# Accumulator tiles for four up products, later Gelus and a later second softmax, and gate multiplications left to the scheduler, in a PEER decoder layer

## The chip, the cores and the metric

The kernel runs on one core of a Trainium2 chip. The metric is the device time of one execution in microseconds, taken as the median of the runs.

## The reference

One hybrid decoder layer over 256 tokens with 16 meta tokens ahead of them and a width of 2048, all in float32. The token-mixing half is a layer norm, an input projection, a causal pooling mixer, a gated short convolution, a gated merge and an output projection. The channel-mixing half is a PEER layer, which retrieves single-neuron experts by product keys; the change concerns this half alone:

```
q = (xb @ w_q).reshape(PEER_BLOCK, PEER_HEADS, 2, PEER_HALF)
s1 = einsum("thc,hnc->thn", q[:, :, 0], keys_1)
s2 = einsum("thc,hnc->thn", q[:, :, 1], keys_2)
v1, i1 = top_k(s1, 16)
v2, i2 = top_k(s2, 16)
...
top_s, sel = top_k(cand_s, 16)
gate = softmax(top_s)
act = gelu(einsum("td,tkd->tk", xb, expert_u[idx]))
coef = gate * act
return einsum("tk,tkd->td", coef, expert_v[idx])
```

There are 128 x 128 = 16384 experts, 8 heads, and 16 experts for each head and token.

## The kernel before

The kernel does not gather expert rows for most tokens. For the first TD = 224 tokens it multiplies all 16384 experts with the tokens and weights each product with a gate, which is zero for an expert that the token did not choose. The experts come in 128 groups of 128, and `e` counts the groups. The last 32 tokens are computed from gathered rows ("lone" rows).

**Splitting.** A float32 weight tile `raw` (1 MB, three buffers) comes by a DMA that SyncE (SP) issues (`load`, L82 to L85). In two halves it is split into a rounded part `whi` (a cast on ACT, L95) and a rest `wlo` (a subtraction, L74, on DVE or POOL); each has three buffers. TensorE (PE) multiplies both parts.

**up(e)** (L627) is the first product, of group e's rows of expert_u with the 224 tokens: 32 matmuls (L108, L109) into one PSUM tile of the pool `mm`, which has four buffers and also serves the query products, the transposes and the gate products. Afterwards `both` (L111) copies one half of the result to `gl` (ACT, L112) and adds the other (DVE, L113). The Gelu (ACT, L625) is put off: `gelus(late)` leaves the `late` newest tiles for later. The first LEAD = 44 ups run ahead of the second products; both their `wlo` halves are made by POOL.

**The gates.** The query products are finished by `q_done`, which finds the top 16 on DVE (lines 438 to 512). `finish(t)` (L514) makes the softmax of token tile t: a subtraction (DVE, L522), an Exp (ACT, L526), a sum, a reciprocal and a multiplication (DVE, L531), and then three PE transposes (L545). It is begun after the ups that ROUTED names and goes on by one step at every half up. Then `gates` builds one-hot matrices on DVE and multiplies them on PE (L595), and a copy of the gates goes to memory (`spill`), 7 pieces of 32 tokens.

**The down phase** has 32 blocks of NB = 4 groups (the loop at L782). For a block, `fetch` (L742) reads its gates `G` back with 7 DMAs of 64 KB on SP's queue, into one of two buffers. `coef(e)` (L644) multiplies `gl` with `G` (DVE, L648) and splits it into `c_hi` (ACT, L77) and `c_lo` (DVE, L74). `down(es, dh)` multiplies with two 1 MB tiles of expert_v for each half dh of the output: 48 matmuls for 4 groups (L660). Two further ups stand ahead of each `down` until all 128 are done, so the last blocks run without ups. The gathers of lone rows lie in between.

**What sets the order.** A tile framework schedules the program by priorities and by the order in which it is written; each engine and each DMA queue then runs its instructions in one fixed order. Two statements steer it: `tc.high_priority(offset)` pulls the casts ahead, and `tc.issue_after(instruction)` binds an instruction behind another that stands earlier on its engine. `last_on["dve"]` is the latest `wlo` or `both` addition on DVE.

Of the kernel before, what the change touches and what calls it, by code (L numbers as in the profile page):

```python
# [35 lines left out]
NB = 4  # L36
NBLK = NKEY // NB
AHEAD = 80
UAHEAD = 100
LEAD = 44  # L40
ROUTED = (3, 6)
GT = 8
TG = 32
LONE = 32
TD = T - LONE
# [8 lines left out]
def block(ctx, tc, x, meta, w_in, small, pool_w, projs, w_out, wq, keys, eu, eur, ev,  # L54
          ln1_g, ln1_b, ln2_g, ln2_b, lin_g, lin_b, out):
    nc = tc.nc
# [10 lines left out]
    def ps_mm():  # L67
        return mm.tile([P, 512], F32, name="mm")

    def ps_acc(t, c):  # L70
        return accp.tile([P, 512], F32, name=f"acc{t}{c}")
# [4 lines left out]
    def split(hi, lo, full):  # L76
        nc.scalar.copy(hi, full)  # L77
        lo_part(lo, full, hi)
# [3 lines left out]
    def load(src, shape=None):  # L82
        t = raws.tile([P, 2, 1024], F32, name="raw")
        last_load[0] = nc.sync.dma_start(t if shape is None else shape(t), src).ins
        return t  # L85

    last_lo = [None]
    last_on = {}

    def halves(parts, raw, lo_eng=None, lo_eng1=None, ahead=AHEAD):  # L90
        for s in range(2):
            hi = parts.tile([P, 1024], F32R, name="whi")
            lo = parts.tile([P, 1024], F32R, name="wlo")
            with tc.high_priority(offset=ahead):
                last_on["act"] = nc.scalar.copy(hi, raw[:, s]).ins  # L95
                eng = lo_eng1 if s and lo_eng1 else lo_eng
                last_lo[0] = lo_part(lo, raw[:, s], hi, eng)
                last_on["pool" if eng is nc.gpsimd else "dve"] = last_lo[0].ins
            yield hi, lo
# [6 lines left out]
    def mm2(ps, whi, wlo, xhl, first, last):  # L106
        n = xhl.shape[-1]
        nc.tensor.matmul(ps[:, :2 * n].rearrange("p (s t) -> p s t", s=2), whi, xhl, start=first, stop=False)  # L108
        nc.tensor.matmul(ps[:, :n], wlo, xhl[:, 0], start=False, stop=last)  # L109

    def both(dst, ps, n):  # L111
        nc.scalar.copy(dst, ps[:, n:2 * n])  # L112
        last_on["dve"] = nc.vector.tensor_tensor(dst, dst, ps[:, :n], op=OP.add).ins  # L113
# [46 lines left out]
    def step():  # L160
        for g in list(waiting):
            if next(g, 1) == 1:
                waiting.remove(g)
# [6 lines left out]
    with ExitStack() as pa:  # L170
# [38 lines left out]
        for t in range(NT):  # L209
            t0, n = (META + P, P) if t else (0, META + P)  # L210
            for k0 in range(0, KD, 2):
                ps = ps_acc(k0 // 2 % 2, k0 // 4 % 2).rearrange("p (k t) -> p k t", k=2)
# [123 lines left out]
        for m in range(KD):  # L336
# [10 lines left out]
            for (hi, lo), y in zip(halves(parts, praw), (ya, yb)):  # L347
                ps = ps_mm()
# [207 lines left out]
    with ExitStack() as pb:  # L556
# [13 lines left out]
        def gates():  # L570
            def hots(t0):
                shape = [P, GT, P]
                i_, j_, g_ = (v[:, ..., t0:t0 + GT, None].to_broadcast([*v.shape[:-1], GT, P])
                              for v in (i_T, j_T, g_T))
                B = ohp.tile(shape, F16, name="B")
                nc.vector.tensor_tensor(B, iota_ps[:, None, :].to_broadcast(shape), j_, op=OP.is_equal)
                Ag = ohp.tile([P, 2, GT, P], F16, name="Ag")
                half = [P, GT // 2, P]
                for h in range(2):
                    hs = slice(h * GT // 2, (h + 1) * GT // 2)  # L580
                    A = ps_acc(1, h).rearrange("p (t i) -> p t i", t=GT // 2)
                    nc.vector.tensor_tensor(A, iota_ps[:, None, :].to_broadcast(half), i_[:, hs], op=OP.is_equal)
                    for n in range(2):
                        nc.vector.tensor_tensor(Ag[:, n, hs], A, g_[:, n, hs], op=OP.mult)
                return Ag, B

            def product(t0, Ag, B):
                n, o = divmod(t0, TG)
                if o == 0:
                    wide[0] = ohp.tile([P, NKEY, TG], F32, name="wide")  # L590
                for h in range(2):
                    ps = ps_mm()
                    for u in range(4):
                        for m in range(2):
                            nc.tensor.matmul(ps[:, u * P:(u + 1) * P], B[:, h * 4 + u], Ag[:, m, h * 4 + u],  # L595
                                             start=m == 0, stop=m == 1)
                    nc.scalar.mul(wide[0][:, :, o + h * 4:o + h * 4 + 4],
                                  ps.rearrange("p (t i) -> p i t", t=4), 1.0 / UP)
                if o + GT == TG:
                    put = nc.gpsimd.dma_start(spill[n], wide[0])  # L600
                    with tc.issue_after(put.ins):
                        for g, eng in ((n - 1, nc.gpsimd), (n if n == NG - 1 else -1, nc.sync)):
                            for b in range(2 if g >= 0 else 0):
                                eng.dma_start(Gs[b][:, g], spill[g][:, b * NB:(b + 1) * NB])

            iota_ps = ps_acc(0, 0)[:, :P]
            nc.vector.tensor_copy(iota_ps, iota)
            wide = [None]
            before = None
            for t0 in range(0, TD, GT):  # L610
                if before:
                    product(*before)
                before = (t0, *hots(t0))
                yield
            product(*before)
# [5 lines left out]
        def gelus(left):  # L621
            while len(acts) > left:
                gl = acts.pop(0)
                with tc.issue_after(last_on["act"]):
                    nc.scalar.activation(gl, gl, AF.Gelu)  # L625

        def up(e, lo_engs, ahead=AHEAD, late=0):  # L627
            raw = load(eu[e], lambda t: t.rearrange("p a b -> p (a b)"))
            ps = ps_mm()
            for s, (hi, lo) in enumerate(halves(parts, raw, *lo_engs, ahead)):  # L630
                for kk in range(8):
                    k = s * 8 + kk
                    cs = slice(kk * P, (kk + 1) * P)
                    mm2(ps, hi[:, cs], lo[:, cs], x_hl[:, k, :, :TD], k == 0, k == KD - 1)
                yield
            gl = gelp.tile([P, TD], F32, name="gl")
            both(gl, ps, TD)
            acts.append(gl)
            gelus(late)
            gels[e] = gl  # L640
# [3 lines left out]
        def coef(e):  # L644
            gl = gels.pop(e)
            glv = gl.rearrange("p (g t) -> p g t", t=TG)
            with tc.issue_after(last_on["dve"]):
                nc.vector.tensor_tensor(glv, glv, Gs[e // NB][:, :, e % NB], op=OP.mult)  # L648
            c_hi = coefp.tile([P, TD], F32R, name="c_hi")
            c_lo = coefp.tile([P, TD], F32R, name="c_lo")  # L650
            split(c_hi, c_lo, gl)
            coefs[e] = (c_hi, c_lo)
# [86 lines left out]
        ahead, rate, credit = iter(()), 0.0, 0.0  # L739
# [7 lines left out]
        def tick(gen):  # L747
            nonlocal credit, lone_credit
            for _ in gen:
                step()  # L750
                lone_credit += lone_rate
                while lone_credit >= 1:
                    lone_credit -= 1
                    next(lone_work, None)
                credit += rate
                while credit >= 1:
                    credit -= 1
                    next(ahead, None)

        for e in range(LEAD):  # L760
            tick(up(e, (nc.gpsimd, nc.gpsimd), UAHEAD, 3))
            if e in ROUTED:
                waiting.append(finish(ROUTED.index(e)))
            if e == ROUTED[1] + 3:
                while waiting:
                    step()
                ahead, rate = gates(), (TD // GT + 1) / (2 * (LEAD - 7 - e))
        for _ in ahead:
            pass
        gelus(0)  # L770
# [11 lines left out]
        for e0 in range(0, NKEY, NB):  # L782
            es = range(e0, e0 + NB)
            if e0 and es[-1] < NKEY - 1:
                fetch(e0 // NB + 1)
            for e in es:
                coef(e)
            for dh in range(2):
                for _ in range(NB // 2):
                    if n_up < NKEY:  # L790
                        tick(up(n_up, (None, nc.gpsimd)))
                        n_up += 1
                if dh == 0 or es[-1] < NKEY - 1:
                    tick(down(es, dh))
# [106 lines left out]
```

## Time and profile before

| | us |
|---|---|
| median of 3 runs | 2117.13 (2116.28 to 2117.24) |
| the profiled execution | 2117.67 |
| its span in the trace | 2115.9 |
| PE busy | 2054.7 (97%) |
| DVE busy | 1525.5 (72%) |
| ACT busy | 1001.8 (47%) |
| POOL busy | 600.8 (28%) |

The span runs from the first to the last instruction that the profiler records. How the rows in the section further down are read: a window row names the stretch in us, its length, then the busy time and the count of instructions of PE, of PE's weight loads (PEld), DVE, ACT and POOL, then the granted TensorE clock as a share of full speed, the DMA engines' busy share, and GB/s. A timeline row has the start in us, the duration (of all its instructions, where x is over 1), engine, line, operation, output <- inputs, shapes and count; in square brackets stands the idle time before it and what ended it. A group row has the busy time in us, the mean in ns, the idle time before these instructions and the releaser to which most of it goes. A row of the chain has the start, the duration, and what ran. SPq is SP's DMA queue.

### The profile page before, as it was taken

The page shows a single profiled execution, that of the slowest core. Times are in us where ns is not written, and L with a number is a line of the kernel's source. Part 1 is how long each engine was busy: PE and PEld are TensorE (multiplying, and loading weights), DVE is VectorE, ACT ScalarE, POOL GpSimd, SP SyncE. Part 2 cuts the span into 40 slices and gives each one's busy share as a digit, 9 for nine tenths or more (in the row PEclk, how much of TensorE's full clock was granted, in tenths as well). Part 3 has the DMA queues.
Part 4 walks back from the last instruction along what each step waited for, and adds up shares of the span by engine and source line. Part 5 has one row for each costly group of instructions (what it writes and reads, how often), then busy time and mean ns, then how long its engine had stood idle before and what let it go on. Part 6 is the DMA issues. An engine that isn't in the chain of part 4 may idle for free.

```text
span 2115.9 us, 29922 instructions
## 1 busy us (share of the span) xinstructions
PE 2054.7 (97%) x11558; PEld 1770.5 (84%) x11558; DVE 1525.5 (72%) x2340; ACT 1001.8 (47%) x1424; POOL 600.8 (28%) x294
## 2 busy tenths in 40 slices
PE   7999999999999699999999999999999999999997
PEld 6999888888888689998888888888888888877765
DVE  7766666666779878836767776776677677788878
ACT  5444544444443356554444444444444445444442
POOL 0000000000065588883332333232334232300001
PEclk9999999999999799999999999999999999999998
DMA  5555555566553357787878777878787877877654
GB/s 202 219 180 182 195 181 191 187 224 233 191 183 125 107 202 273 264 284 274 292 266 291 272 269 268 291 269 289 262 283 268 293 260 275 278 271 270 224 169 158
DMA packets 114334, 498.09 MB, mean 235 GB/s; under 512 B 11200, under 2 KB 38336, under 8 KB 73344
## 3 DMA queue, kind: packets, MB, share of 16 engines
q1 hardware_dynamic: 103584, 413.61, 56.8%
q0 software_dynamic: 10608, 82.58, 10.0%
q8 instruction: 90, 1.47, 0.3%
q14 instruction: 52, 0.43, 0.1%
HBM read 478.32 MB, written 16.78 MB: 234 GB/s over the span
## 4 chain that ended last, share of the span: by engine, by line
PE 90%; DVE 7%; issue 1%; DMA 1%; POOL 1%; ACT 1%; SPq 0%; POOLq 0%; ACTq 0%
PE mm L108 28%; PE acc L660 27%; PE mm L109 14%; PE mm L660 5%; PE mm L103 2%; PE mm L102 2%; PE mm L104 2%; PE acc L116 2%; PE acc L117 2%; PE acc L118 2%; PE mm L595 1%; POOL wlo L74 1%; DMA raw<-in_eu 0%; DVE res L669 0%; PE acc L219 0%
## 5 line engine op out<-in xcount | busy, mean ns | idle before, releaser
L95 ACT CAST whi<-raw 128x1024 fp32r<-128x1024 f32 x738 | 772.2, 1048 | 801.5 <-PE mm L108 256.4
L74 DVE TENSOR_TENSOR wlo<-raw,whi 128x1024 fp32r<-128x1024 f32 x546 | 684.7, 1257 | 471.8 <-ACT whi L95 468.3
L108 PE MATMUL mm<-x_hl,whi 128*128 128x448 f32 x2048 | 656.1, 379 | 18.6 <-DVE gl L113 16.8
L74 POOL TENSOR_TENSOR wlo<-raw,whi 128x1024 fp32r<-128x1024 f32 x192 | 490.9, 2563 | 587.1 <-ACT whi L95 282.9
L109 PE MATMUL mm<-x_hl,wlo 128*128 128x224 f32 x2048 | 544.4, 266 | 6.3 <-POOL wlo L74 6.1
L108 PEld LDWEIGHTS mm<-x_hl,whi 128*128 128x128 f32 x2048 | 387.7, 189 | 50.4 <-issue 17.2
L109 PEld LDWEIGHTS mm<-x_hl,wlo 128*128 128x128 f32 x2048 | 394.9, 193 | 10.3 <-POOL wlo L74 8.0
L660 PE MATMUL acc<-whi,c_lo 128*128 128x512 f32 (+1 forms) x832 | 260.7, 395 | 5.0 <-DVE c_lo L74 5.0
L660 PE MATMUL acc<-whi,c_hi 128*128 128x512 f32 (+1 forms) x832 | 260.8, 395 | 4.3 <-ACT c_hi L77 4.3
L660 PE MATMUL acc<-wlo,c_hi 128*128 128x512 f32 (+1 forms) x832 | 260.7, 395 | 0.0
L108 PE MATMUL mm<-h_hl,whi 128*128 128x512 f32 x640 | 225.0, 395 | 0.0
L136 POOL TENSOR_TENSOR rstd<-rstd,neghalf 128x1 f32<-128x1 f32 (+1 forms) x7 | 5.8, 821 | 713.8 <-DVE rstd L135 697.5
L660 PEld LDWEIGHTS acc<-whi,c_lo 128*128 128x128 f32 (+1 forms) x832 | 146.4, 176 | 52.7 <-DVE c_lo L74 6.4
L660 PEld LDWEIGHTS acc<-wlo,c_hi 128*128 128x128 f32 (+1 forms) x832 | 146.2, 176 | 46.1 <-issue 0.2
L660 PEld LDWEIGHTS acc<-whi,c_hi 128*128 128x128 f32 (+1 forms) x832 | 143.0, 176 | 47.5 <-ACT c_hi L77 4.8
L109 PE MATMUL mm<-h_hl,wlo 128*128 128x256 f32 x640 | 180.5, 282 | 0.0
L669 DVE SCALAR_TENSOR_TENSOR res<-res,acc 128x512 f32<-128x512 f32 x208 | 131.6, 679 | 22.6 <-PE acc L660 20.7
L108 PEld LDWEIGHTS mm<-h_hl,whi 128*128 128x128 f32 x640 | 120.4, 188 | 26.9
L625 ACT ACTIVATE gl<-gl 128x224 f32<-128x224 f32 x128 | 49.7, 389 | 168.8 <-DVE gl L113 168.8
L109 PEld LDWEIGHTS mm<-h_hl,wlo 128*128 128x128 f32 x640 | 121.3, 189 | 0.0
L103 PE MATMUL mm<-h_hl,whi 128*128 128x258 f32 (+3 forms) x384 | 110.4, 288 | 0.0
L102 PE MATMUL mm<-h_hl,whi 128*128 128x258 f32 (+3 forms) x384 | 109.3, 285 | 0.0
(189 smaller groups left out, 2586.4 us busy)
## 6 DMA issues: line engine op xcount, KB each, us to landing
raw<-in_eu SPq DMA_DIRECT2D x128, 1024.0 KB, 6.0
raw<-in_ev SPq DMA_DIRECT2D x128, 1024.0 KB, 5.6
raw<-in_w_in SPq DMA_DIRECT2D x64, 1024.0 KB, 4.9
raw<-in_projs SPq DMA_DIRECT2D x16, 1024.0 KB, 4.9
raw<-in_w_out SPq DMA_DIRECT2D x16, 1024.0 KB, 5.0
raw<-in_wq SPq DMA_DIRECT2D x16, 1024.0 KB, 4.8
spill<-wide POOLq DMA_DIRECT2D x7, 2048.0 KB, 7.9
G<-spill SPq DMA_DIRECT2D x212, 64.0 KB, 5.1
```

Source lines behind the costliest of these rows:

```text
L74: return (eng or nc.vector).tensor_tensor(lo, full, hi.bitcast(F32), op=OP.subtract)
L95: last_on["act"] = nc.scalar.copy(hi, raw[:, s]).ins
L102: nc.tensor.matmul(ps, whi, xhi, start=first, stop=False)
L103: nc.tensor.matmul(ps, whi, xlo, start=False, stop=False)
L104: nc.tensor.matmul(ps, wlo, xhi, start=False, stop=last)
L108: nc.tensor.matmul(ps[:, :2 * n].rearrange("p (s t) -> p s t", s=2), whi, xhl, start=first, stop=False)
L109: nc.tensor.matmul(ps[:, :n], wlo, xhl[:, 0], start=False, stop=last)
L116: nc.tensor.matmul(ps, xhi, whi, start=first, stop=False)
L117: nc.tensor.matmul(ps, xhi, wlo, start=False, stop=False)
L625: nc.scalar.activation(gl, gl, AF.Gelu)
L660: nc.tensor.matmul(ps[c][:n_t], c_[:, ts], v_[:, c * 512:(c + 1) * 512], start=e == first and n == 0, stop=e == last and n == 2)
L669: nc.vector.scalar_tensor_tensor(r, r, 1.0 if (t, dh, c) in added else ALPHA, ps[c][:n_t], op0=OP.mult, op1=OP.add)
```

## The change

```
-ROUTED = (3, 6)
+ROUTED = (3, 7)
+LATE = 8
...
         def up(e, lo_engs, ahead=AHEAD, late=0):
             raw = load(eu[e], lambda t: t.rearrange("p a b -> p (a b)"))
-            ps = ps_mm()
+            ps = ps_acc(e // 2, e % 2) if e < 4 else ps_mm()
...
         def coef(e):
             gl = gels.pop(e)
             glv = gl.rearrange("p (g t) -> p g t", t=TG)
-            with tc.issue_after(last_on["dve"]):
+            with tc.issue_after(last_on["dve"]) if e < 2 * NB else ExitStack():
                 nc.vector.tensor_tensor(glv, glv, Gs[e // NB][:, :, e % NB], op=OP.mult)
...
         for e in range(LEAD):
-            tick(up(e, (nc.gpsimd, nc.gpsimd), UAHEAD, 3))
+            tick(up(e, (nc.gpsimd, nc.gpsimd), UAHEAD, LATE))
             if e in ROUTED:
                 waiting.append(finish(ROUTED.index(e)))
             if e == ROUTED[1] + 3:
                 while waiting:
                     step()
-                ahead, rate = gates(), (TD // GT + 1) / (2 * (LEAD - 7 - e))
+                ahead, rate = gates(), (TD // GT + 1) / (2 * (LEAD - 6 - e))
```

Ups 0 to 3 now accumulate in the four PSUM tiles that the down phase uses later (`ps_acc`). The Gelus of the lead stay eight ups behind rather than three. The second softmax begins after up 7 rather than up 6, and the gate products start one up later at the same rate. The gate multiplications of blocks 0 and 1 remain bound behind the latest DVE instruction; those of all later blocks are free to be scheduled as early as the scheduler sees fit. From line 41 on, a line number of the changed kernel is higher by one.

**First place: ACT's order about the first softmax.** The `whi` tiles are casts, of up 3's second half (`whi_6676`) and of the ups behind it; `gl_6558` belongs to up 0, `gl_6604` to up 1, and `gt` is the first softmax. Before:

```order
L112 COPY gl_6604<-mm_6563 128x224
L95 CAST whi_6676<-raw_6653 128x1024
L625 ACT_TABLE_LOAD
L625 ACTIVATE gl_6558<-gl_6558 128x224
L95 CAST whi_6703<-raw_6700 128x1024
```

and after:

```order
L113 COPY gl_6604<-acc01_6563 128x224
L96 CAST whi_6676<-raw_6653 128x1024
L96 CAST whi_6702<-raw_6699 128x1024
L113 COPY gl_6650<-acc10_6609 128x224
L96 CAST whi_6724<-raw_6699 128x1024
L96 CAST whi_6750<-raw_6747 128x1024
L113 COPY gl_6696<-acc11_6655 128x224
L96 CAST whi_6770<-raw_6747 128x1024
L527 ACT_TABLE_LOAD
L527 ACTIVATE gt_6722<-gt_6722 128x128
L96 CAST whi_6797<-raw_6794 128x1024
```

The first Gelu has left this place; it now stands behind the first half of up 8. The Exp of the first softmax comes with no Gelu ahead of it, directly in front of the casts of up 6 (`whi_6797`). On PE the transposes of this softmax stand behind up 6 in both kernels.

**Second place: DVE's order in the first block of the down phase.** `raw_9662` and `raw_9696` are block 0's two tiles of expert_v (dh 0), `raw_9737` is up 46's; `gl_6945` and the three next to it are block 2's, `gl_7203` and its followers block 3's. Before:

```order
L74 TENSOR_TENSOR wlo_9665<-raw_9662,whi_9664 128x1024
L113 TENSOR_TENSOR gl_9605<-gl_9605,mm_9564 128x224
L74 TENSOR_TENSOR wlo_9681<-raw_9662,whi_9680 128x1024
L74 TENSOR_TENSOR wlo_9699<-raw_9696,whi_9698 128x1024
L113 TENSOR_TENSOR gl_9654<-gl_9654,mm_9611 128x224
L74 TENSOR_TENSOR wlo_9718<-raw_9696,whi_9717 128x1024
L74 TENSOR_TENSOR wlo_9741<-raw_9737,whi_9740 128x1024
```

and after:

```order
L75 TENSOR_TENSOR wlo_9665<-raw_9662,whi_9664 128x1024
L114 TENSOR_TENSOR gl_9605<-gl_9605,mm_9564 128x224
L649 TENSOR_TENSOR gl_6945<-gl_6945,G_9911 128x224
L649 TENSOR_TENSOR gl_6993<-gl_6993,G_9911 128x224
L649 TENSOR_TENSOR gl_7064<-gl_7064,G_9911 128x224
L649 TENSOR_TENSOR gl_7124<-gl_7124,G_9911 128x224
L75 TENSOR_TENSOR wlo_9681<-raw_9662,whi_9680 128x1024
L75 TENSOR_TENSOR wlo_9699<-raw_9696,whi_9698 128x1024
L114 TENSOR_TENSOR gl_9654<-gl_9654,mm_9611 128x224
L649 TENSOR_TENSOR gl_7203<-gl_7203,G_10287 128x224
L75 TENSOR_TENSOR wlo_9718<-raw_9696,whi_9717 128x1024
L649 TENSOR_TENSOR gl_7281<-gl_7281,G_10287 128x224
```

The multiplications of block 2 and block 3 now stand inside block 0, between the `wlo` subtractions that PE needs for block 0. Blocks 4 to 14 follow in the same way within the next two blocks.

**Third place: SP's queue, in the same stretch.** `G_9911` is the fetch of block 2, `G_10287` that of block 3; the numbered `spill` pieces are its 7 DMAs. Before, from the first fetch's last pieces on:

```order
L84 DMA raw_9737<-in_eu 128x2048
L745 DMA G_9911<-spill4_6434 128x128
L745 DMA G_9911<-spill5_6435 128x128
L745 DMA G_9911<-spill6_6436 128x128
L84 DMA raw_9785<-in_eu 128x2048
L84 DMA raw_9836<-in_ev 128x2x1024
L84 DMA raw_9872<-in_ev 128x2x1024
```

and after:

```order
L85 DMA raw_9737<-in_eu 128x2048
L746 DMA G_9911<-spill4_6434 128x128
L746 DMA G_9911<-spill5_6435 128x128
L746 DMA G_9911<-spill6_6436 128x128
L746 DMA G_10287<-spill0_6430 128x128
L746 DMA G_10287<-spill1_6431 128x128
L746 DMA G_10287<-spill2_6432 128x128
L746 DMA G_10287<-spill3_6433 128x128
L85 DMA raw_9785<-in_eu 128x2048
L746 DMA G_10287<-spill4_6434 128x128
L746 DMA G_10287<-spill5_6435 128x128
L746 DMA G_10287<-spill6_6436 128x128
```

Block 3's fetch has moved ahead of the weight tile of up 47 (`raw_9785`) and directly behind block 2's. Both fetches use the same G buffer, so the second waits for block 2's multiplications.

## Rows read from the trace of the kernel before

**Rows 1.** The page, busy time and share of each engine.

```profile
PE 2054.7 (97%) x11558; PEld 1770.5 (84%) x11558; DVE 1525.5 (72%) x2340; ACT 1001.8 (47%) x1424; POOL 600.8 (28%) x294
```

**Rows 2.** Busy time of each engine in four stretches.

```profile
660.00:770.00 110.00, 86.81 (x503) 79.73 (x502) 92.74 (x288) 47.03 (x74) 64.12 (x27) 0.88 0.35 118
960.00:1000.00 40.00, 39.18 (x205) 32.80 (x204) 28.64 (x38) 20.42 (x31) 13.35 (x8) 1.00 0.82 299
1000.00:1800.00 800.00, 800.00 (x4247) 681.52 (x4246) 564.35 (x691) 380.47 (x532) 275.19 (x126) 1.00 0.78 276
2000.00:2050.00 50.00, 43.88 (x174) 32.41 (x173) 37.55 (x46) 21.31 (x25) 0.00 (x0) 0.90 0.54 179
```

**Rows 3.** Timeline of PE in the routing stretch.

```profile
706.38 0.71 PE L108 MATMUL mm<-x_hl,whi 128*128 128x448 f32 x1 [14.15 <-DVE gl L113]
736.37 0.27 PE L545 MATMUL mm<-ident,gt 128*128 128x128 f32 x1
```

**Rows 4.** Timeline of ACT in the routing stretch, the first Gelu.

```profile
706.27 0.39 ACT L625 ACTIVATE gl<-gl 128x224 f32<-128x224 f32 x1 [14.20 <-DVE gl L113]
```

**Rows 5.** Timeline of DVE in the routing stretch.

```profile
662.34 0.24 DVE L485 TENSOR_TENSOR cs<-v 128x112 f32<-128x112 f32 x1
...
678.07 2.51 DVE L485 TENSOR_TENSOR cs<-v 128x112 f32<-128x112 f32 x1
...
703.33 0.28 DVE L522 TENSOR_TENSOR gt<-top 128x128 f32<-128x128 f32 x1
...
727.91 0.29 DVE L531 TENSOR_TENSOR gt<-gt,sums 128x128 f32<-128x128 f32 x1
```

**Rows 6.** Timeline of POOL in the routing stretch.

```profile
673.39 11.81 POOL L74 TENSOR_TENSOR wlo<-raw,whi 128x1024 fp32r<-128x1024 f32 x5 [17.55 <-PE acc L118]
...
707.67 2.37 POOL L74 TENSOR_TENSOR wlo<-raw,whi 128x1024 fp32r<-128x1024 f32 x1 [14.46 <-ACT whi L95]
```

**Rows 7.** Timeline of SP's queue where block 0 begins.

```profile
961.24 1.76 SPq L745 DMA_DIRECT2D G<-spill  x4
...
964.24 1.51 SPq L745 DMA_DIRECT2D G<-spill  x3
```

**Rows 8.** Tile G, the seven DMAs issued from 961 to 966 us.

```profile
L745 SPq DMA_DIRECT2D G<-spill x7: 339/423/562, 961.2 to 965.2; - x7
...
DMA to landing us min/median/max: 1.9/2.7/9.7
```

**Rows 9.** Tile G, the DMAs issued from 964.5 to 965.5 us.

```profile
DMA to landing us min/median/max: 5.1/7.4/9.7
```

**Rows 10.** Tile G, all fetches from 1100 to 2000 us.

```profile
DMA to landing us min/median/max: 1.8/5.2/9.6
```

**Rows 11.** Timeline of DVE in block 0 of the down phase.

```profile
965.16 0.37 DVE L113 TENSOR_TENSOR gl<-gl,mm 128x224 f32<-128x224 f32 x1
...
966.93 2.36 DVE L74 TENSOR_TENSOR wlo<-raw,whi 128x1024 fp32r<-128x1024 f32 x2 [1.40 <-ACT whi L95]
...
996.03 1.29 DVE L648 TENSOR_TENSOR gl<-gl,G 128x224 f32<-128x224 f32 x4
```

**Rows 12.** Timeline of PE, block 0's second group of experts.

```profile
969.51 0.62 PE L660 MATMUL acc<-wlo,c_hi 128*128 128x512 f32 x2
```

**Rows 13.** The chain that ended last, in order of time.

```profile
966.45 11.08 PE acc L660 x48
...
987.55 11.10 PE acc L660 x48
...
2031.85 13.43 PE acc L660 x48
```

**Rows 14.** Groups of PE instructions in the down phase.

```profile
L660 PE MATMUL acc<-whi,c_lo 128*128 128x512 f32 (+1 forms) x832 | 260.7, 395 | 5.0 <-DVE c_lo L74 5.0
L660 PE MATMUL acc<-whi,c_hi 128*128 128x512 f32 (+1 forms) x832 | 260.8, 395 | 4.3 <-ACT c_hi L77 4.3
```

**Rows 15.** Timeline of PE near the end.

```profile
2031.85 1.22 PE L660 MATMUL acc<-whi,c_hi 128*128 128x512 f32 x2 [4.30 <-ACT c_hi L77]
```

More of the change, by code (lines that the diff above doesn't have):

```diff
@@ L40 @@
 LEAD = 44
-ROUTED = (3, 6)
+ROUTED = (3, 7)
+LATE = 8
 GT = 8
@@ L628, in up @@
             raw = load(eu[e], lambda t: t.rearrange("p a b -> p (a b)"))
-            ps = ps_mm()
+            ps = ps_acc(e // 2, e % 2) if e < 4 else ps_mm()
             for s, (hi, lo) in enumerate(halves(parts, raw, *lo_engs, ahead)):
@@ L646, in coef @@
             glv = gl.rearrange("p (g t) -> p g t", t=TG)
-            with tc.issue_after(last_on["dve"]):
+            with tc.issue_after(last_on["dve"]) if e < 2 * NB else ExitStack():
                 nc.vector.tensor_tensor(glv, glv, Gs[e // NB][:, :, e % NB], op=OP.mult)
@@ L760, in block @@
         for e in range(LEAD):
-            tick(up(e, (nc.gpsimd, nc.gpsimd), UAHEAD, 3))
+            tick(up(e, (nc.gpsimd, nc.gpsimd), UAHEAD, LATE))
             if e in ROUTED:
@@ L766, in block @@
                     step()
-                ahead, rate = gates(), (TD // GT + 1) / (2 * (LEAD - 7 - e))
+                ahead, rate = gates(), (TD // GT + 1) / (2 * (LEAD - 6 - e))
         for _ in ahead:
```

## The prediction, made before the changed kernel ran

> **What bounds the kernel now.** I read the page first. PE is busy 97% of the span, DVE 72%, ACT 47% and POOL 28% [rows 1]: TensorE bounds this kernel, and an edit pays only where PE stops. So I cut the span into stretches [rows 2]; look at the second number of each row against its length. From 1000 to 1800 us PE is busy in all 800.00 of 800 us, at a granted clock of 1.00: nothing can be gained there, and every wait put there is paid in full. PE stops in two places that this change touches. From 660 to 770 us, where routing and the first ups run side by side, it is busy 86.81 of 110 us; near the end, from 2000 to 2050 us, 43.88 of 50, with the clock at 0.90. Then I asked the timelines what ended the stops. In the first place PE waits 14.15 us, until 706.38, for an addition on DVE that frees a PSUM tile of the pool `mm` [rows 3], and ACT stands 14.20 us in its first Gelu for the same addition, with weight casts queued behind it [rows 4]. In the second, the groups of line 660 show 5.0 us of idle time released by `c_lo` and 4.3 us by `c_hi` [rows 14], the largest single stop being 4.30 us [rows 15]: the coefficients of blocks without ups are late.
>
> A measurement of this kernel can tell about 0.2%, 4.2 us, from no change. The sum is made against the profiled execution, 2117.67 us, which is 0.54 us above the median of 2117.13.
>
> **A. Routing: accumulator tiles, later Gelus, later softmax.** Ups 0 to 3 no longer take `mm` tiles, and no Gelu stands ahead of the casts. So the stop of 14.15 us [rows 3] goes from where it is. What is late next? On PE the first softmax's transposes stand behind up 6 in both orders, and they need the multiplication at line 531, which ends at 727.91 + 0.29 = 728.2 [rows 5]. PE reached its transpose at 736.37 [rows 3], so with DVE unchanged at most 8.2 us can be gained. But DVE won't be unchanged. POOL, which makes `wlo` for these ups, was idle for 14.46 us before 707.67 [rows 6]; now it gets work. The same instruction of line 485 takes 0.24 us with POOL idle, and 2.51 us while POOL ran its subtractions [rows 5, 6]. Of the routing chain's instructions of this kind (a subtraction, an addition or a cast with all its operands in SBUF) I take four to fall newly beside POOL's work: 4 x 2.3 = 9.2 us, which takes the softmax from 728.2 to 737, about where PE is anyway. Besides, the Exp now stands ahead of up 6's casts on ACT, and its input is ready only at 703.33 + 0.28 [rows 5]. I take −1 us. Ends: −8 with no such contention; +8 if it hits twice as many instructions and PE stands at up 6 as it stood at up 3. The middle is taken since the long form of line 485 is what the trace shows whenever POOL works.
>
> **B. End of the lead.** Five more Gelus are put off to its end, 5 x 0.39 = 1.95 us on ACT [rows 4], and the gate products end one up later. The casts of the next weights can slip behind them by that much; PE has its own ups to do in that time. +1, between 0 and 3.
>
> **C. The start of the down phase.** This is the large term. Unbound multiplications are issued on DVE long ahead of need, and a DVE instruction that waits holds all behind it. In the new order block 2's four stand inside block 0, in front of a `wlo` that PE needs at 969.51 [rows 12]. They wait for block 2's fetch.
>
> *Round 1.* The fetch is issued as before, from 961.24, the last piece at 965.2 [rows 7, 8]. The seven land after 1.9 to 9.7 us [rows 8]; the last three, behind a 1 MB weight tile in the queue, after 5.1 to 9.7 [rows 9]. DVE gets there at 965.16 + 0.37 [rows 11] and waits until 965.2 + 9.7 = 974.9; four multiplications, 1.29; one `wlo`, 2.36 / 2 = 1.18 [rows 11]: 977.4. PE stops 977.4 − 969.5 = 7.9 us.
>
> *Round 2.* Block 3's fetch goes to the same buffer, so it starts at 974.9 + 1.3 = 976.2. Seven issues take 1.76 + 1.51 = 3.3 us [rows 7], one weight tile's lies between (0.3), and the landing I take at 5.1, the least behind a weight tile [rows 9] and the median of later fetches, 5.2 [rows 10]: 984.9. One multiplication and one `wlo` more: 986.4. PE wants it at 969.5 + 7.9 for the second group, and two groups later at 2.77 each (11.08 / 4 [rows 13]), 982.9: 3.5 us.
>
> *Round 3* (block 4) falls beside two ups, which give PE 10.0 us (987.55 − 966.45 − 11.08 [rows 13]) against 3.3 + 5.1 + 1.3 = 9.7: nothing. *Round 4* (block 5) has seven issues in a row and stands between the first two `wlo` of a `down`: 8.4 us less what PE has in hand there, one group and the part of the next that needs no `wlo`, some 4.4: 4 us.
>
> *The other nine* (blocks 6 to 14) alternate between both buffers, since block 1's multiplications then free the second: 9.7 / 2 = 4.9 us each, with about one weight tile per set in SP's queue; PE uses one tile per 21.1 / 4 = 5.3 us [rows 13]. Hidden, just; DMA engines are busy 0.78 to 0.82 here [rows 2], so I take 0.8 us each, 7 in all, between 0 and, with each landing at 9.7, (14.3 / 2 − 5.3) x 9 = 17.
>
> *Clock.* The 48 matmuls behind the 4.30 us stop took 13.43 us instead of 11.08 [rows 13, 15]; a stop of 7.9 us should cost this too: 2.4.
>
> C = 7.9 + 3.5 + 4 + 7 + 2.4 = +25. The lower end has every piece landing in 2.7 us [rows 8]: 965.2 + 2.7 + 1.3 + 1.2 = 970.4 against 969.5, 1 us, and nothing else, so 2. The upper end, all at 9.7: 7.9 + 8 + 9 + 17 + 2.4 = 44.
>
> What these sums rest on is a DMA's time. The Trainium skill, "DMA: Bandwidth & Descriptors", section "Anatomy of one DMA — SWDGE (gpsimd) path", gives about 2.0 us fixed plus bytes over 436 GB/s, an estimate of 2.15 us for 64 KB from that page; by it C would be that lower end. The four fast landings agree with it, 1.9 to 2.7 us [rows 8]; the three behind a weight tile, 5.1 to 9.7 [rows 9], do not.
>
> **D. The tail.** With the multiplications done long before, `c_hi` and `c_lo` are no longer behind them: 5.0 + 4.3 = 9.3 us of stops [rows 14] go, and the slow 48 matmuls come back to 11.08, 2.4 us [rows 13]. −12; ends −14 (one more block regains its clock) and −5 (the casts stay late for another reason, such as a coefficient buffer that PE still reads). In the middle blocks the early multiplications gain nothing, since PE waits for nothing there [rows 2].
>
> **Sum.** −1 + 1 + 25 − 12 = +13: 2117.67 + 13 = 2130.7, and against the median 2130.
>
> **The rivals.**
>
> *R1, faster: fetches land in time.* If the early queue drains so that all G pieces land in 2.7 us, as the first four do [rows 8], DVE's waits hide. −1 + 1 + 2 − 12 = −10: about 2107, and 2100 if A also gains its 8. For it: while SP stands for a buffer it issues no weight tiles, so fewer bytes compete. Against it: round 1's fetch is issued with the same tiles around it as before, and its last three landed late [rows 9]. It decides at the landing of block 2's last piece: before 968 this rival holds. Chance 0.23.
>
> *R2, the same: only the first stops cost.* Rounds 1 and 2 and the clock, 13.8, and all later sets hide: −1 + 1 + 13.8 − 11.7 = +2: 2119, within 0.2%. For it: PE's 5.3 us a tile against my 4.9 per set. 0.16.
>
> *R3, much slower: weight tiles starve.* SP issues in order, so a fetch that waits for multiplications holds the weight tiles behind it. At the upper end C is 44: −1 + 1 + 44 − 12 = +32: 2149. For it: landings of up to 9.6 us occur in later fetches as well [rows 10]. Against: the median there is 5.2. 0.09.
>
> **How the numbers follow.** The forecast, slower at 2130, has 0.52; its own range, with C from 17 to 41, is 2122 to 2146. Faster is R1, 0.23; the same is R2, 0.16; slower is the forecast and R3, 0.61. The range of 2107 to 2146 leaves out R3 and the lower half of R1, 0.2 together.
>
> **What the changed profile would show.** Right: PE with no stop of 14 us near 706 but with the transposes of line 546 still at about 736; near 969 a PE stop of 7 to 9 us at line 661 released by a `wlo` on DVE, with DVE idle before line 649 and released by a DMA of G; one or two more of 3 to 5 us within 50 us; clock under 1.00 from 960 to 1000; from 1800 on no idle time released by `c_lo` or `c_hi`. Wrong: PE busy throughout 960 to 1100 (R1); PE idle before line 109 for weight tiles (R3); stops of `c_hi` still in the tail, with D near nothing.

## The result, and the profile after

The changed kernel takes 2132.64 us, the median of 6 runs (2131.39 to 2134.43), against 2116.05 us before (2114.09 to 2117.24): a ratio of 1.008 with a 95% interval of 1.0067 to 1.0093. It is slower by 16.6 us, where +13 and 2130 were forecast. The profiled execution took 2134.43 us, its span is 2132.6.

The windows of the changed kernel, in the same columns as [rows 2]:

```profile
660.00:770.00 110.00, 89.92 (x530) 82.43 (x529) 90.82 (x289) 46.83 (x72) 69.53 (x29) 0.91 0.36 126
...
960.00:1000.00 40.00, 27.76 (x131) 22.28 (x132) 21.89 (x29) 11.33 (x15) 9.45 (x6) 0.87 0.67 229
1000.00:1100.00 100.00, 87.88 (x426) 71.84 (x425) 74.27 (x104) 38.27 (x55) 26.29 (x13) 0.93 0.76 254
1100.00:1800.00 700.00, 700.00 (x3722) 595.88 (x3721) 506.46 (x605) 337.71 (x468) 230.03 (x110) 1.00 0.79 276
...
2000.00:2050.00 50.00, 50.00 (x219) 37.91 (x218) 44.56 (x48) 28.15 (x31) 0.00 (x0) 1.00 0.61 202
```

PE now stops for 12.2 us between 960 and 1000 and for 12.1 between 1000 and 1100, where it stopped for 0.8 and nothing. From 2000 to 2050 it is busy throughout, where it stopped for 6.1 us. The middle is as before. The groups of line 661 (660 before) say the same of the whole span; the idle time stands behind the bar:

```profile
L661 PE MATMUL acc<-wlo,c_hi 128*128 128x512 f32 (+1 forms) x832 | 262.7, 397 | 17.9 <-DVE wlo L75 17.9
L661 PE MATMUL acc<-whi,c_lo 128*128 128x512 f32 (+1 forms) x832 | 261.6, 395 | 0.0
L661 PE MATMUL acc<-whi,c_hi 128*128 128x512 f32 (+1 forms) x832 | 261.1, 395 | 0.0
```

The waits for `c_lo` and `c_hi` [rows 14] are gone, and 17.9 us for `wlo` have come. The timelines of DVE and of SP's queue in block 0 of the changed kernel show how, first DVE:

```profile
961.38 0.37 DVE L114 TENSOR_TENSOR gl<-gl,mm 128x224 f32<-128x224 f32 x1
971.32 1.30 DVE L649 TENSOR_TENSOR gl<-gl,G 128x224 f32<-128x224 f32 x4 [9.57 <-issue]
972.54 2.35 DVE L75 TENSOR_TENSOR wlo<-raw,whi 128x1024 fp32r<-128x1024 f32 x2
...
980.59 0.39 DVE L649 TENSOR_TENSOR gl<-gl,G 128x224 f32<-128x224 f32 x1 [5.41 <-DMA G<-spill]
```

then SP:

```profile
957.45 1.76 SPq L746 DMA_DIRECT2D G<-spill  x4
960.07 0.33 SPq L85 DMA_DIRECT2D raw<-in_eu  x1
960.46 13.94 SPq L746 DMA_DIRECT2D G<-spill  x7
974.50 0.37 SPq L85 DMA_DIRECT2D raw<-in_eu  x1
```

DVE reaches block 2's multiplications at 961.7 and stands idle for 9.57 us; SP stands in the middle of the next fetch until these multiplications free the buffer. The timeline names no releaser for that wait ("issue" is time for which it shows none); the view of tile G from 960 to 962 us, which holds the fetch's last three pieces, does (who waited for it, in us and times, then the landing):

```profile
  DVE gl L649: 9.6, 1
...
DMA to landing us min/median/max: 7.4/7.4/7.4
```

PE's timeline shows what that costs, in seven of its stops:

```profile
973.81 1.22 PE L661 MATMUL acc<-wlo,c_hi 128*128 128x512 f32 x2 [7.88 <-DVE wlo L75]
982.17 0.73 PE L661 MATMUL acc<-wlo,c_hi 128*128 128x512 f32 x2 [0.22 <-DVE wlo L75]
...
986.42 0.37 PE L110 MATMUL mm<-x_hl,wlo 128*128 128x224 f32 x1 [1.46 <-DVE wlo L75]
...
994.28 0.37 PE L110 MATMUL mm<-x_hl,wlo 128*128 128x224 f32 x1 [2.58 <-DVE wlo L75]
...
1006.67 1.22 PE L661 MATMUL acc<-wlo,c_hi 128*128 128x512 f32 x2 [4.07 <-DVE wlo L75]
...
1030.55 1.22 PE L661 MATMUL acc<-wlo,c_hi 128*128 128x512 f32 x2 [3.07 <-DVE wlo L75]
1037.43 1.22 PE L661 MATMUL acc<-wlo,c_hi 128*128 128x512 f32 x2 [2.49 <-DVE wlo L75]
```

Look at the durations too. A pair of the matmuls of line 661 takes 0.62 us at full clock; right behind the stops of 7.88, 4.07, 3.07 and 2.49 us it takes 1.22, and the next pair 1.05. Windows of 2 us show the granted clock there (the first number behind the five engines):

```profile
974.00:976.00 2.00, 2.00 (x5) 1.52 (x6) 1.19 (x2) 0.78 (x2) 0.00 (x0) 0.50 0.74 153
...
1038.00:1040.00 2.00, 2.00 (x6) 1.48 (x5) 2.00 (x4) 0.00 (x0) 0.00 (x0) 0.50 0.84 209
...
1052.00:1054.00 2.00, 2.00 (x9) 1.82 (x8) 2.00 (x2) 0.97 (x1) 0.00 (x0) 0.50 0.96 365
```

PE is busy all the time in these, at 0.50: the lower of its two levels, 1.2 instead of 2.4 GHz.

**Three pieces of the difference.** One place in each kernel splits the span. PE came to the `wlo` product of block 0's second group at 969.51 [rows 12], and had not to wait for it; it now comes there at 973.81 − 7.88 = 965.93, where the wait begins, so the lead gives 3.6 us. The first block without ups stands in the chain of both kernels, before:

```profile
1834.26 8.83 PE mm L660 x37
```

and after:

```profile
1865.20 8.76 PE mm L661 x37
```

That is 30.9 us later, so the down phase to this point loses 30.9 + 3.6 = 34.5. The span ends 16.7 later (2132.6 − 2115.9), so the tail gives 14.2.

### The profile page after: what moved, and what is told of

Read it like the earlier page. It is cut to its first block, busy times and chain, and to the rows that moved or that the text cites. A ratio compares the mean times of both kernels' runs of the same rounds, so it can differ in the third digit from the quotient of the medians.

```text
span 2132.6 us, 29945 instructions
## 1 busy us (share of the span) xinstructions
PE 2059.7 (97%) x11558; PEld 1769.5 (83%) x11558; DVE 1548.4 (73%) x2340; ACT 1007.4 (47%) x1423; POOL 589.0 (28%) x294
## 4 chain that ended last, share of the span: by engine, by line
PE 87%; DVE 9%; issue 2%; DMA 1%; SPq 1%; POOL 0%; ACT 0%; DVEq 0%; POOLq 0%; ACTq 0%
PE mm L109 28%; PE acc L661 25%; PE mm L110 14%; PE mm L661 6%; PE mm L104 2%; PE mm L103 2%; PE mm L105 2%; PE acc L117 2%; PE acc L118 2%; PE acc L119 2%; PE mm L596 1%; DVE wlo L75 1%; DMA G<-spill 1%; DVE eq L515 1%; DVE eq L513 1%
## 5 line engine op out<-in xcount | busy, mean ns | idle before, releaser
L75 POOL TENSOR_TENSOR wlo<-raw,whi 128x1024 fp32r<-128x1024 f32 x192 | 484.7, 2531 | 619.5 <-ACT whi L96 338.2
L109 PE MATMUL mm<-x_hl,whi 128*128 128x448 f32 x1984 | 635.8, 379 | 2.7 <-ACT whi L96 2.7
L110 PE MATMUL mm<-x_hl,wlo 128*128 128x224 f32 x1984 | 526.3, 265 | 10.6 <-DVE wlo L75 6.3
L109 PEld LDWEIGHTS mm<-x_hl,whi 128*128 128x128 f32 x1984 | 375.4, 189 | 34.6 <-ACT whi L96 3.0
L110 PEld LDWEIGHTS mm<-x_hl,wlo 128*128 128x128 f32 x1984 | 381.6, 192 | 15.1 <-DVE wlo L75 7.7
L661 PE MATMUL acc<-wlo,c_hi 128*128 128x512 f32 (+1 forms) x832 | 262.7, 397 | 17.9 <-DVE wlo L75 17.9
```

The source lines that it names most:

```text
L75: return (eng or nc.vector).tensor_tensor(lo, full, hi.bitcast(F32), op=OP.subtract)
L661: nc.tensor.matmul(ps[c][:n_t], c_[:, ts], v_[:, c * 512:(c + 1) * 512], start=e == first and n == 0, stop=e == last and n == 2)
```

## The experiments

In each the median stands against that of the kernel before, run on the same chip; "the lead's part" means everything in the change except the unbound multiplications.

**1. The lead's part alone.** The multiplications bound again:

```
-            with tc.issue_after(last_on["dve"]) if e < 2 * NB else ExitStack():
+            with tc.issue_after(last_on["dve"]):
```

> The lead's part of the change alone (accumulator tiles, eight late Gelus, later second softmax); all gate multiplications bound as before. My theory: the down phase pays nothing and the tail gains nothing, so what is left is the lead alone. Block 0's first wait for a wlo ended at 969.51 us before and began at 973.81 - 7.88 = 965.93 in the changed kernel, 3.6 us earlier, so 2116.0 - 3.6 = about 2112.5; PE's stop of 14 us before line 109 is replaced by one of 10 to 13 us before the transposes of line 546; from 1000 to 1100 us PE is busy 100 of 100. Rival: the eight late Gelus and the shifted gate products lengthen the end of the lead or the first blocks and take part in the loss: 2116 or more.

Measured: 2113.97 against 2116.64, ratio 0.9988 (0.9979 to 0.9997). The lead alone gives 2.7 us, and PE's stop of 14 us has become one of 12.88 us before the transposes of line 546. PE is busy 39.99 of 40 us from 960 and 100 of 100 from 1000. The rival falls: the lead has no share in the loss.

**2. The unbound multiplications alone.** The kernel before with this line of the change only:

```
-            with tc.issue_after(last_on["dve"]):
+            with tc.issue_after(last_on["dve"]) if e < 2 * NB else ExitStack():
```

> The freed gate multiplications alone, with the lead as before. My theory: the loss at the start of the down phase (34.5 us in the changed kernel, from block 0 to the first block without ups) and the gain in the tail (14.2 us) both belong to this part: 2116.0 + 34.5 - 14.2 = about 2136. Rival: the loss needs the lead's changes as well (the queue stands otherwise at block 0): under 2126, with the first stop of PE in block 0 under 4 us.

Measured: 2135.55 against 2116.64, ratio 1.0090 (1.0076 to 1.0103), +18.9 for the +20 expected. PE's first stop in block 0 is 8.26 us. In its trace the first block without ups stands at 1865.71 us, 31.5 later than before, and the span ends 17.3 later, so the tail gives 14.2 here too. Loss and tail gain both belong to this line.

**3. Two blocks only.** The changed kernel, unbound in blocks 2 and 3 alone:

```
-            with tc.issue_after(last_on["dve"]) if e < 2 * NB else ExitStack():
+            with tc.issue_after(last_on["dve"]) if not 2 * NB <= e < 4 * NB else ExitStack():
```

> The changed kernel with only blocks 2 and 3 unbound (groups 8 to 15); all others bound. My theory: each set of four multiplications pays for its own fetch, so the first stops of the changed kernel come back as they were (7.9 us, then 0.2 and 1.5), with some 4 us of lower clock behind them, and nothing after 1000 us; no gain in the tail: 2112.5 + 13.6 = about 2126. Rival: the loss is one of the weight tiles, which stand in SP's queue behind many fetches; with two sets there is little of that: 2112 to 2116, with no stop over 3 us.

Measured: 2130.31 against 2116.64, ratio 1.0070 (1.0056 to 1.0084). PE's timeline in this kernel:

```profile
972.52 1.22 PE L661 MATMUL acc<-wlo,c_hi 128*128 128x512 f32 x2 [8.14 <-DVE wlo L75]
...
980.73 0.73 PE L661 MATMUL acc<-wlo,c_hi 128*128 128x512 f32 x2 [0.78 <-DVE wlo L75]
984.98 0.37 PE L110 MATMUL mm<-x_hl,wlo 128*128 128x224 f32 x1 [1.47 <-DVE wlo L75]
992.84 0.37 PE L110 MATMUL mm<-x_hl,wlo 128*128 128x224 f32 x1 [2.57 <-DVE wlo L75]
```

The same stops at the same places, none after 1000. Two sets of thirteen cost 13.0 us of stops and, against the lead's part alone, 2130.31 − 2113.97 = 16.3 in all. The time is 4 us above the 2126 expected, which counted 9.6 us of stops and 4 of lower clock. Many fetches in SP's queue are not needed for the loss.

**4. The burst in another place.** Bound up to group 83, unbound from there (`if e < 84 else ExitStack()`):

> The changed kernel with the gate multiplications unbound from group 84 on, where the last blocks (21 to 31) begin to be served; blocks 0 to 20 bound. In DVE's order eleven sets now stand close together among the last ups. My theory: the loss goes with the burst, wherever it stands, since each set waits in DVE's queue for a fetch that was issued just ahead of it: the stretch from 1000 to 1100 us is free of stops, and stops of 2 to 8 us released by wlo on DVE appear some 100 to 150 us ahead of the first block without ups, 20 to 30 us together with the clock; the tail's gain of 14 stays: 2114 + 25 - 14 = about 2125. Rival: the loss belongs to the start of the down phase, where the weight tiles have no lead; then nothing is lost: 2100.

Measured: 2126.00 against 2115.09, ratio 1.0048 (1.0033 to 1.0063). PE's timeline in this kernel, its largest stops:

```profile
1772.56 1.22 PE L661 MATMUL acc<-wlo,c_hi 128*128 128x512 f32 x2 [4.88 <-DVE wlo L75]
...
1799.62 0.73 PE L661 MATMUL acc<-wlo,c_hi 128*128 128x512 f32 x2 [3.26 <-DVE wlo L75]
...
1828.14 1.17 PE L661 MATMUL acc<-wlo,c_hi 128*128 128x512 f32 x2 [3.38 <-DVE wlo L75]
```

From 960 to 1100 us PE is busy throughout; from 1767 to 1858 it stops for 19 us in all, and the time is near the 2125 expected. The loss has moved with the burst; it does not belong to the start of the down phase. The largest stop is smaller than the 7.88 of block 0, though.

**5. The gathers of lone rows moved.** What else makes block 2's pieces late? This is the view of the DMA queues of the changed kernel from 957 to 975 us: busy tenths in 40 slices of 0.45 us, then packets, MB and share by queue:

```profile
DMA  9975545139389998999899999999510000000444
...
q1 hardware_dynamic: 1737, 2.27, 37.5%
q0 software_dynamic: 288, 2.10, 27.8%
```

The second queue carries 2.10 MB: two gathers of lone rows, issued by POOL. From 962 us on the DMA engines are nearly full until about 969.6, from 970.5 they are idle, and DVE's wait ends at 971.32. So the changed kernel with the gathers begun two blocks later:

```
-        lone_work, lone_rate = lone_rows(), (4 * NU + 4) / LONE_TICKS
...
+            if e0 == 2 * NB:
+                lone_work, lone_rate = lone_rows(), (4 * NU + 4) / (LONE_TICKS - 32)
```

> The changed kernel, with the gathers of lone rows begun two blocks later (at block 2, at a rate that ends them at about the same place). DVE's and SP's order in blocks 0 and 1 stays that of the changed kernel, but the two 1 MB gathers that ran beside block 2's fetch are gone from there. My theory: block 2's last pieces land late because the DMA engines have the gathers and the weight tiles to move as well; without the gathers they land some 3 to 5 us earlier, and PE's first stop falls from 7.9 to under 5 us, the whole kernel by 3 to 6: 2127 to 2130. Rival: the pieces are late behind the weight tile in SP's own queue alone; the first stop stays at 7 to 8.5 us, and the time at 2132.

Measured: 2120.54 (10 runs, 2114.97 to 2122.07) against 2115.99, ratio 1.0019 (1.0010 to 1.0029). Its profile is of the shortest run, 2114.97, so its rows are those of a good run, 5.6 us under the median. DVE's and PE's timelines there:

```profile
965.13 1.30 DVE L649 TENSOR_TENSOR gl<-gl,G 128x224 f32<-128x224 f32 x4 [4.07 <-DMA G<-spill]
```

```profile
967.62 1.22 PE L661 MATMUL acc<-wlo,c_hi 128*128 128x512 f32 x2 [2.39 <-DVE wlo L75]
```

and in the queues from 957 to 975 us the second one is absent, while the median landing of G's pieces is 2.0 us (2.5 in the changed kernel):

```profile
q1 hardware_dynamic: 2394, 3.32, 56.6%
...
G<-spill SPq DMA_DIRECT2D x14, 64.0 KB, 2.0
```

The first stop falls from 7.88 to 2.39 us, more than expected, and the median time by 12, twice the best that was expected: PE is busy 96.65 of 100 us from 1000 to 1100 as well (87.88 in the changed kernel). The rival, the weight tile alone, falls. But the edit moves more than the gathers: DVE's work on the gathered rows (line 696, 2.28 us each, from 986.28 on in the changed kernel) goes with them. The first stop lies ahead of that work, so there it is the gathers; how much of the rest of the 12 us is theirs is not shown. The Trainium skill, "DMA: Bandwidth & Descriptors", section "Issuing engines are not separate DMA queues", says that transfers started by different engines run on the same 16 DMA engines and interleave; the runs agree: DVE went on 9.9 us after the issue of the last piece (961.4) with POOL's gathers beside it, and 4.4 us after it (960.7) without them.

**6 and 7. What the lead gains by.** The accumulator tiles alone, in the kernel before:

```
-            ps = ps_mm()
+            ps = ps_acc(e // 2, e % 2) if e < 4 else ps_mm()
```

> Only the accumulator tiles for ups 0 to 3; Gelus, softmax and gate multiplications as before. My theory: two waits for the same DVE addition stood one behind the other, PE's for a tile of the pool mm and ACT's in the first Gelu, and this takes the first alone. PE does one more up (5 us) and then stops until about 708 for a weight cast that stands behind the Gelu: the 14 us stop released by the addition becomes one of about 9 us released by a cast (ACT whi). The transposes still follow the softmax's multiplication, so the time stays within 3 us of before (2114 to 2117). Rival: the tiles alone are what the lead gains by, the Gelu is beside the path: no stop over 5 us before 715, and the time of the lead part, 2114 or less.

Measured: 2116.39 against 2115.09, ratio 1.0008 (0.9999 to 1.0018). And the later Gelus alone (`UAHEAD, 3` to `UAHEAD, 8`):

> Only the later Gelus (eight ups behind); tiles, softmax and gate multiplications as before. My theory: PE's wait for the addition that frees a tile of mm stays as it was, 14 us until about 706, or longer, since POOL and ACT now work on and DVE's instructions become slower; the time is that of before or up to 5 us more (2116 to 2121). Rival: the Gelu in ACT's queue is the real wait and the tile's is only named by the profile: the stop shrinks to 9 us or less, and the time falls below 2114.

Measured: 2119.87 against 2115.09, ratio 1.0021 (1.0012 to 1.0030). The stops of PE, with the tiles alone:

```profile
708.01 0.74 PE L108 MATMUL mm<-x_hl,whi 128*128 128x448 f32 x1 [9.49 <-ACT whi L95]
```

and with the Gelus alone:

```profile
708.85 0.71 PE L108 MATMUL mm<-x_hl,whi 128*128 128x448 f32 x1 [16.11 <-DVE gl L113]
...
728.39 0.71 PE L108 MATMUL mm<-x_hl,whi 128*128 128x448 f32 x1 [7.46 <-DVE gl L113]
```

Take away the wait for the tile, and the Gelu in ACT's queue is late next; take away the Gelu, and the tile's wait remains and grows. Neither edit gains anything alone, as expected; the Gelus alone lose 5 us. The two together without the later second softmax were not run, so what that adds to the lead's 2.7 us is open.

**8 to 10. The gain without the loss.** The multiplications bound as before, but written half a block earlier. `gate` is the multiplication taken out of `coef`:

```
             for e in es:
+                if e0 == 0:
+                    gate(e)
                 coef(e)
             for dh in range(2):
+                if dh and es[-1] < NKEY - 1:
+                    for e in es:
+                        gate(e + NB)
```

With the lead's part:

> The lead's part of the change, with the gate multiplications of each block bound behind the latest DVE instruction as before, but written half a block earlier (between the two halves of the block before). My theory: the loss comes from multiplications whose fetch has not landed, and the tail's gain from multiplications that are done before the block begins; half a block (11 us, or 21 with ups) is more than a fetch's 5 us, so the gain comes without the loss: 2116.0 - 3.6 - 14.2 = about 2098, no stop over 1 us from 1000 us to the last block. Rival: the tail's stops are those of the coefficient casts themselves and stay: 2112.

Measured: 2099.95 against 2116.64, ratio 0.9926 (0.9913 to 0.9940), the best time so far and near the 2098 expected. The windows of this kernel at both places:

```profile
960.00:1000.00 40.00, 39.85 (x208) 33.62 (x209) 28.22 (x37) 18.91 (x27) 14.95 (x9) 1.00 0.84 304
...
2000.00:2050.00 50.00, 50.00 (x219) 37.93 (x218) 44.01 (x61) 26.04 (x30) 0.00 (x0) 1.00 0.61 199
```

Without the lead's part, and with it once more:

> The kernel before, with nothing changed but the gate multiplications of a block, which are written half a block earlier (still bound behind the latest DVE instruction). My theory: the tail's stops go, 9.3 us and the clock behind them, 14 in all, and nothing is paid for it: before - 14 = about 2102; the stop of 14 us near 706 stays. Rival: part of the gain of the kernel with the lead's part came from the two together; then under 10 us are gained here: 2106 or more.

> The lead's part and the earlier multiplications once more, on the same chip as the two beside it. My theory: 3 us under the kernel with the earlier multiplications alone, as the lead's part alone was 2.7 under before. Rival: the lead's part adds nothing: the same time within 1 us.

Measured: 2102.55 (ratio 0.9933, 0.9920 to 0.9947) and 2100.57 (0.9927, 0.9913 to 0.9940), both against 2116.81. The tail gives 14.3 us by itself. What the lead adds, 2.0 us, is of the size expected, but the intervals overlap.

**11 and 12. One more up ahead of the transposes.** `ROUTED = (4, 7)` in the kernel of experiment 8, run twice:

> The kernel with the multiplications half a block earlier, and the first softmax begun after up 4 rather than up 3, so that its transposes stand behind up 7. My theory: PE's stop of 13.5 us before the transposes, which is left in every kernel with the lead's part, is filled by one more up: 5 us, less 1 or 2 for slower DVE instructions: 2100 - 4 = about 2096, the stop before line 546 at 8 to 10 us. Rival: the softmax's own instructions on ACT and DVE move back with it, or up 7 waits for a tile of mm that DVE's additions free late: 2099 to 2103.

> The same with the first softmax begun after up 4, once more beside the other. It stops 16.7 us for a tile of mm where the other stops 13.5 us for the softmax. My theory: the time is that of the kernel beside it within 1 us, since both wait for DVE's work in the end. Rival: it is 2 us less, as the two medians taken on different chips would have it.

Measured: 2097.97 against 2115.09 (0.9918, 0.9905 to 0.9932) and 2098.61 against 2116.81 (0.9914, 0.9900 to 0.9927), beside 2100.57 for experiment 8's on the same chip. PE's timeline:

```profile
738.20 0.69 PE L546 MATMUL mm<-ident,ij 128*128 128x128 f32 x2 [16.67 <-DVE gl L114]
```

PE does the extra up, and then waits 16.67 us (12.99 in the second run's profile) for a tile of `mm`, close to the rival's way. On the same chip the median is 2.0 us lower; in the first run, against the kernel before on its own chip, it is 17.1 us under it where experiment 8 was 16.7. The intervals overlap; whether it gains stays open. The best two versions beat both kernels: 2098 to 2100.

## Why the prediction was right, and where its terms were off

The sign, the mechanism and the place were right: unbound multiplications wait on DVE for fetches that were issued just ahead of them, `wlo` stands behind, and PE stops in block 0. The sum, +13, came out as +16.7 between the profiled spans. That it came so near is in part luck: A and B came out 3.6 us lower than forecast, C 9.5 higher and D 2.2 lower, and these misses partly cancel.

**A and B** were forecast at 0 together and gave 3.6 us in the trace, 2.7 as a run of its own. The stop did move to the transposes:

```profile
734.25 0.47 PE L546 MATMUL mm<-ident,gt 128*128 128x128 f32 x1 [12.71 <-DVE gt L532]
```

The softmax was to be ready at 737, 9 us later than before, for four slow instructions; its multiplication ended at 734.19, 6.0 later than the 728.2 of before, and PE went on at 734.25. That DVE slows beside POOL's new work can be read from one instruction, line 502, which takes ten times as long while POOL works (DVE's timeline of the changed kernel):

```profile
688.99 2.19 DVE L502 TENSOR_TENSOR rc<-rc,far 128x64 f32<-128x64 f32 x1
...
722.20 0.23 DVE L502 TENSOR_TENSOR rc<-rc,far 128x64 f32<-128x64 f32 x1
```

No run took POOL's work away, so the cause is argued from the two rows and not shown.

**C** was forecast at 25 and was 34.5. The stops add up to nearly what was worked out, 24.3 against 22.4, but not place by place: round 1 was 7.9 and is 7.88; round 2 was 3.5 and is 0.22; up 46 and up 47, for which nothing was counted, stop for 1.46 and 2.58; round 4 was 4 and is 4.07; the other nine were 7 and are 8.05 (0.54, 3.07, 2.49, 0.20 and 1.75). That these misses nearly cancel is luck. Three of these stops (1.46, 2.58 and 1.75) end with a `wlo` that took 3.3 to 3.4 us on DVE rather than 1.2, each begun while POOL ran a subtraction, and so are not waits for a fetch alone. The one behind 2.58, with POOL at work from 990.05 to 993.14:

```profile
990.89 3.33 DVE L75 TENSOR_TENSOR wlo<-raw,whi 128x1024 fp32r<-128x1024 f32 x1
```

The term that was mis-sized is the one called *Clock*: 2.4 us, counted for one stop. The clock fell behind five stops (7.88, 4.07, 3.07, 2.49 and 1.75 us). Each pair of line 661 then came 0.85 us after the last rather than 0.46; summed over the slow matmuls this makes 2.4, 1.5, 1.5, 1.5 and 1.6, or 8.5 us. Some 2 us of C are left without a place.

Round 1 was right for a reason that was half right. The forecast said that the last three pieces land late "behind a 1 MB weight tile". Experiment 5 shows that the two gathers on the other queue did most of it: without them the wait on DVE is 4.07 instead of 9.57 us with the same weight tile in the queue. It also decides how the page's rule was to be weighed, that of "Anatomy of one DMA — SWDGE (gpsimd) path" in the Trainium skill's "DMA: Bandwidth & Descriptors", which is given for DMAs that GpSimd issues, while SP issues these pieces: its estimate of 2.15 us describes the median piece without gathers (2.0 us in experiment 5), but neither the last one there, for which DVE waited until 4.4 us after its issue, nor those beside 2 MB of gathers.

**D** was forecast at −12 and gave −14.2; experiment 9 gives −14.3 for it alone. It lies at the end of its range, for the reason that the forecast named there: one more block regains its clock. In the chain of the kernel before, 40 matmuls behind a stop of 1.61 us ran at full pace, and 40 behind one of 1.83 us, in the same place of a later block, took 1.6 us more (granted clock 0.50 from 2006 to 2009):

```profile
1868.72 9.47 PE acc L660 x40
...
2005.47 11.04 PE acc L660 x40
```

With the stops and the block that was counted this makes 9.3 + 2.4 + 1.6 = 13.3; 0.9 us were not traced.

**The rivals.** R1, fetches in time, fell at its own point, 968 us: DVE went on at 971.32. R2, only the first stops, fell too: rounds from 1000 us on cost 12.1 us of stops. R3's starved weight tiles would show as waits of ACT for a DMA of `raw`. In the view of waits of the changed kernel from 960 to 1060 us (us, times, longest) there is none, but DVE waits for G:

```profile
DVE gl L649 <- DMA G<-spill: 19.0, 4, 8.2
...
DVE gl L649 <- issue: 9.6, 1, 9.6
```

and two sets without a long queue (experiment 3) already cost 16.3 us.

## What to carry to other kernels

Freeing an instruction from its place frees it to stand early in an in-order queue, where its own wait becomes the wait of everything behind it; before unbinding, ask when its input lands and what the queue holds after it. Where an input needs a few microseconds of lead, give it a fixed lead (here half a block): this took the tail's 14 us and paid nothing. Where two waits end with the same event, neither edit alone need show a gain, and a short stop can cost more than its length, by the slow clock behind it.

## What the runs showed that was not expected

Two gathers of 1 MB each, issued by POOL, held pieces of 64 KB on SP's queue: with the work on lone rows begun two blocks later, DVE's first wait falls from 9.57 to 4.07 us and the changed kernel from 2132.64 to 2120.54. The lower clock came after stops as short as 1.75 and 2.49 us here, while the stop of 2.58 us ahead of 994.28 was followed by matmuls at full pace (granted clock 1.00 from 994 to 998); the same stop in experiment 3, 2.57 us, was followed by slow ones (0.50 from 994 to 996). The later Gelus, taken alone, made the kernel 5 us slower, by a second stop of 7.46 us for the same pool of tiles.
